# The planned duration of TensorE products is changed in a hand-ordered two-layer decoder kernel

## Chip, cores and metric

The kernel runs on one core of a Trainium2 chip. The metric is the device time of one execution in microseconds (us); lower is better. Engines are named as the profile names them: PE (TensorE matmul), PEld (TensorE weight load), DVE (VectorE), ACT (ScalarE), POOL (GpSimd), SP (SyncE, which issues the weight DMAs).

## What is computed

A decoder trunk of two layers over 256 tokens of width 1024, all in float32. Cut to its shape:

```python
for i in range(2):
    h = h + 0.5 * swiglu(rmsnorm(h), w_ff1_in[i], w_ff1_out[i])          # 1024 -> 2*2816 -> 1024
    u = rmsnorm(h)
    z = u @ w_in[i]             # [q | k | v | forget logits | conv GLU input | gate_attn | gate_conv]
    y_attn = forgetting_attention(q, k, v, f) @ w_attn_out[i]            # 8 heads x 64, causal
    y_conv = silu(rmsnorm(depthwise_conv31(a * sigmoid(b)))) @ w_conv_out[i]
    h = h + (sigmoid(ga) * y_attn + sigmoid(gc) * y_conv) @ w_out[i]
    h = h + 0.5 * swiglu(rmsnorm(h), w_ff2_in[i], w_ff2_out[i])
    h = h + sigmoid(rmsnorm(h) @ w_ple_gate[i]) * (p[i] @ w_ple_proj[i])
out = rmsnorm(h)
```

## The kernel before

Every float32 operand of a large product is split into two parts, high and low (`hi`, `lo`), and a product is three matmuls: high by high, high by low, low by high. Activations are held as `xs` (both parts side by side), weights come by DMA into `raw`, ACT copies the high part out (`whi`), and DVE subtracts it to get the low part (`wlo`). A weight block is mostly handled as two halves, each of 1024 columns per partition, and six half buffers (`WB`) exist for each of `whi` and `wlo`. So each weight half has to pass DMA, ACT and DVE before PE can use it.

The order of the instructions of each engine is written by a planner, the class `Flow`, when the program is built. It keeps a clock for PE, DVE and ACT, charges every operation a duration, and appends the operation that its clocks and priorities pick. `product` places a piece of large products on PE and moves PE's clock by `cost * len(items)`; `sides` lets small PE work (transposes, attention scores, attention values) in between two pieces once the planner believes its inputs are there. The engines then run their queues in exactly that order, each instruction waiting on semaphores for its real inputs; the planner's clocks themselves are not in the program. A duration in the planner therefore changes nothing but positions in the queues.

Three rules of the planner matter here. Splits of weights (`Weights.op`, `prio`) count how far a half is ahead of the half that PE's planned clock is on: less than one half ahead is priority 0.5, less than three (`AHEAD`) is 3, further ahead is 5. The 31 taps of the depthwise convolution are 124 DVE operations of each layer on the accumulator `acc`, with priority 4 (`conv_in`, `taps`): they fill DVE whenever the next halves are three ahead, and give way when they are not. Other DVE work (softmax maxima `nm`, splits of attention outputs) has priority 0 to 2 and goes first.

The mixer of a layer runs these large products in this order: convolution input, first half (`C0`); values and forget logits (`mm_vf`); convolution input, second half (below: C1); four blocks for queries and keys (below Q0, Q1, K0, K1; `mm_b`); eight blocks for the two gates (`mm_a`; the first is below GA0), with attention's scores, transposes and values placed between their pieces; the two output projections; `w_out`. Queries and keys are copied by ACT and then multiplied on POOL (`heads_out`, line 1035). A product on `mm_b` streams 256 columns three times, one on `mm_a` 512 columns three times, one on `mm_vf` 256 and 264 columns three times. The last line that the change touches is the planned duration of `values`, the small products of attention weights and values.

Everything that the helper class `Pinned` issues is recorded under line 285, so rows are told apart by the names of tiles: `mmps` and `xps` are the PSUM banks of PE, `wlo` and `whi` the weight parts, `acc` the convolution's accumulator.

Of the kernel before, what the change touches and what calls it, by code (L numbers as in the profile page):

```python
# [55 lines left out]
PE, V, A = "pe", "vector", "scalar"  # L56
# [7 lines left out]
def ac(n, ptr=0):  # L64
    return 95 + 0.834 * n + 90 * ptr
# [44 lines left out]
class Flow:  # L110
# [9 lines left out]
    def spawn(self, gen, at=None, prio=1, lat=LAT):  # L120
        self.seq += 1
        c = Chain(gen, prio, lat, self.seq)
        self.resume(c, self.t[PE] if at is None else at, None)
        return c.ev
# [290 lines left out]
def trunk(ctx: ExitStack, tc: tile.TileContext, x, p, g_ff1, w_ff1_in, w_ff1_out, g_mix, w_in, b_f,  # L415
# [116 lines left out]
    hT = keep.tile([P, KD, T], F32, name="hT")  # L532


    MB = 3 * 111

    def mm_b(ps, w, cols, xs, start, stop):
        hi, lo = w[0][:, cols], w[1][:, cols]
# [5 lines left out]
    def chunk(bank, m):  # L544
        return bank.t[:, m * T:(m + 1) * T]
# [4 lines left out]
    def items_b(blk, bank, m, k0, ks, kn, xs):  # L550
        return [(blk, k, (chunk(bank, m),), (slice(m * P, (m + 1) * P), xs[:, k0 + k], m == 0 and k0 + k == 0, m == 1 and k0 + k == kn - 1))
                for k in ks]


    def items_1(blk, ps, m, k0, ks, kn, xs):
        return [(blk, k, (ps,), (slice(m * P, (m + 1) * P), xs[:, k0 + k], k0 + k == 0, k0 + k == kn - 1)) for k in ks]


    MA = 3 * 217

    def mm_a(ps, xs, tt, w, start, stop):
        hi, lo = w
# [4 lines left out]


    VF = AW // 2
    MVF = 3 * (111 + 115)  # L570

    def mm_vf(ps, xs, tt, w, start, stop):
        for i, n in enumerate((VF, VF + H)):
# [2 lines left out]
    def piece(mm, cost, items, needs=()):  # L576

        hs = []
        for blk, k, *_ in items:
            if blk.of(k) not in hs:  # L580
                hs.append(blk.of(k))

        def run():
            for blk, k, before, after in items:
                mm(*before, blk.part(k), *after)
        for h in hs:
            wts.use(h)
        product(cost * len(items), run, list(needs) + [h.ready for h in hs])
# [198 lines left out]
    def ffn(wi, wo, norm, nxt, first=None):  # L787
# [3 lines left out]
        for k0 in range(0, KD, step):  # L791
            blks = [wts.take(wi, k0, step, c, 2 * P) for c in (0, FF)]
            for k in range(step):
                for i in range(2):
                    piece(mm_b, MB, [x for m in range(2) for x in items_b(blks[i], banks[i], m, k0, [k], KD, norm.xs)], [norm.ready[k0 + k]])
            wts.release(*blks)
# [3 lines left out]
        with tc.tile_pool(name="ffn", bufs=2) as ph, tc.tile_pool(name="ffn_g", bufs=1) as pg:  # L800
# [18 lines left out]
            for jj in range(KF // 2):  # L819
                if jj:  # L820
                    banks = []
                    for i in range(2):
# [3 lines left out]
                        for m in range(2):  # L826
                            for kk in range(0, KD, 4):
                                piece(mm_b, MB, items_b(blk, bank, m, 0, range(kk, kk + 4), KD, norm.xs))
                        wts.release(blk)
                spawn(glu(jj, *banks))  # L830
            for mm in range(KD // 2):
# [3 lines left out]
                for k0, kc in KPARTS:  # L835
                    blk = wts.take(wo, k0, kc, mm * 2 * P, 2 * P)
                    for m in range(2):
                        for h in blk.halves:
                            ks = range(h.a, h.b)
                            items = items_1(blk, hs[m].t[:, :T], m, k0, ks, KF, gs) if last else items_b(blk, hs[0], m, k0, ks, KF, gs)  # L840
                            piece(mm_b, MB, items, [ready[(k0 + k) // 2] for k in ks])
                        if k0 + kc == KF and last:
# [5 lines left out]
    def block_a(src, xs, kn, c0, needs):  # L848

        banks = [flow.take(mms) for _ in range(TT)]  # L850
        for k0 in range(0, kn, 4):
            blk = wts.take(src, k0, 4, c0, 512)
            for tt in range(TT):
                for h in blk.halves:
                    piece(mm_a_, MA, [(blk, k, (banks[tt].t, xs[:, k0 + k], tt), (k0 + k == 0, k0 + k == kn - 1))
                                      for k in range(h.a, h.b)], [needs[k0 + k] for k in range(h.a, h.b)])
# [6 lines left out]
    def mixer(l, norm, nxt):  # L863
        W = w_in[l]
        norm.root()
        with tc.tile_pool(name="mixer", bufs=1) as ph, tc.tile_pool(name="attn", bufs=2) as at:
# [66 lines left out]
            for k0 in range(0, KD, 4):  # L933
                blk = wts.take(W, k0, 4, V0, AW + H)
                for tt in range(TT):
                    for h in blk.halves:
                        piece(mm_vf, MVF, [(blk, k, (vbs[tt], norm.xs[:, k0 + k], tt), (k0 + k == 0, k0 + k == KD - 1))
                                           for k in range(h.a, h.b)], [norm.ready[k0 + k] for k in range(h.a, h.b)])
# [78 lines left out]
            def heads(c0, dst, scale):  # L1017
                evs = []
                for mm in range(AW // (2 * P)):
                    bank = flow.take(mms)  # L1020
                    blk = wts.take(W, 0, KD, c0 + mm * 2 * P, 2 * P)
                    for m in range(2):
                        for h in blk.halves:
                            ks = range(h.a, h.b)
                            piece(mm_b, MB, items_b(blk, bank, m, 0, ks, KD, norm.xs), [norm.ready[k] for k in ks])
                    wts.release(blk)
# [16 lines left out]
            def softmax(h0, qb, sch):  # L1043
                sc, kl = sch.t, (qb + 1) * P
                xp = yield xps
                pt = xp.t.rearrange("p (h k) -> p h k", h=2)

                def go():
                    for i in range(2):
                        tensor.matmul(out=pt[:, i, :kl], lhsT=QA[:, h0 + i, qb * P:(qb + 1) * P], rhs=KA[:, h0 + i, :kl],  # L1050
                                      start=True, stop=True)
                yield PE, 430 * (qb + 1), go
                yield A, ac(2 * kl), lambda: scalar.copy(out=sc, in_=pt[:, :, :kl])
                xp.free()

                diag = sc[:, :, qb * P:kl]
                nc.gpsimd.affine_select(out=diag, in_=diag, pattern=[[0, 2], [-1, P]], compare_op=ALU.is_ge, fill=NEG,
                                        base=0, channel_multiplier=1)
                yield flow.now + POOL
                nm = small.tile([P, 2], F32, name=f"nm{qb}")  # L1060
                sm = small.tile([P, 2], F32, name=f"sm{qb}")
                yield V, vc(2 * kl), lambda: vector.tensor_reduce(out=nm, in_=sc, axis=AX.X, op=ALU.max, negate=True)

                def exps():
                    for i in range(2):
                        scalar.activation(out=sc[:, i], in_=sc[:, i], func=AF.Exp, bias=nm[:, i:i + 1], accum_out=sm[:, i:i + 1])
                yield A, 2 * (ac(kl, 1) + 97), exps
                yield V, vc(2), lambda: vector.reciprocal(out=sm, in_=sm)

                def norms():  # L1070
                    for i in range(2):
                        scalar.activation(out=sc[:, i], in_=sc[:, i], func=AF.Copy, scale=sm[:, i:i + 1])
                yield A, 2 * ac(kl, 1), norms

            def attention(j):
                for e in have_qk:
                    yield e
                yield max(e.at for e in have_qk) + 2 * QK
                yield have_f
                h0 = 2 * j  # L1080
                sch = []
                for qb in range(TT):
                    h = yield scs[qb]
                    sch.append(h)
                evs = [spawn(softmax(h0, qb, sch[qb]), at=flow.now) for qb in range(TT)]
                for e in evs:
                    yield e
                exp_done[j].at = flow.now
                pT = yield pTs
                pbs = []  # L1090
                for i in range(2):
                    bank = yield mms
                    pbs.append(bank)

                def turned():
                    for i in range(2):
                        for n, part in enumerate((sch[0].t[:, i], sch[1].t[:, i, :P], sch[1].t[:, i, P:])):
                            tensor.transpose(out=pbs[i].t[:, n * P:(n + 1) * P], in_=part, identity=ident)
                yield PE, 660, turned
                for h in sch:  # L1100
                    h.free()
                for i in range(2):
                    yield A, ac(3 * P), lambda: scalar.copy(out=pT.t[:, 3 * i * P:3 * (i + 1) * P], in_=pbs[i].t[:, :3 * P])
                    pbs[i].free()
                yield have_v
                xp = yield xps
                po = xp.t[:, :T]

                def values():
                    for i in range(2):  # L1110
                        vh = slice((h0 + i) * DH, (h0 + i + 1) * DH)
                        o = po[i * DH:(i + 1) * DH]
                        q = pT.t[:, 3 * i * P:3 * (i + 1) * P]
                        tensor.matmul(out=o[:, 0:P], lhsT=v[:, 0, vh], rhs=q[:, 0:P], start=True, stop=True)
                        tensor.matmul(out=o[:, P:T], lhsT=v[:, 0, vh], rhs=q[:, P:2 * P], start=True, stop=False)
                        tensor.matmul(out=o[:, P:T], lhsT=v[:, 1, vh], rhs=q[:, 2 * P:], start=False, stop=True)
                yield PE, 700, values
                pT.free()
                yield from split((os_[:, j, :T], os_[:, j, T:]), po, T)
                xp.free()  # L1120
                os_ready[j].at = flow.now
# [67 lines left out]
            def w_out_part(hs, mm, k0, done=None):  # L1189
                blk = wts.take(w_out[l], k0, KC, mm * 2 * P, 2 * P)  # L1190
                for m in range(2):
                    items = items_b(blk, hs[0], m, k0, range(KC), KD, ms) if len(hs) == 1 else items_1(blk, hs[m].t[:, :T], m, k0, range(KC), KD, ms)
                    piece(mm_b, MB, items, ms_ready[k0 // KC])
                    if done:
# [40 lines left out]
    def ple(l, pT, have_p, norm, nxt, ph):  # L1235
# [8 lines left out]
        for mm in range(KD // 2):  # L1244
            bank = flow.take(mms)
            piece(mm_b, MB, [(blk, k, (chunk(bank, m),), (slice((2 * mm + m) * P, (2 * mm + m + 1) * P), pT[:, k], m == 0 and k == 0, m == 1 and k == 1))
                             for m in range(2) for k in range(2)], [have_p])
# [129 lines left out]
```

## Time and profile before

| | |
|---|---|
| median of 3 runs | 1161.68 us (1161.4 to 1162.49) |
| the profiled execution | 1161.82 us, its span 1160.0 us |
| mean granted TensorE clock | 0.995 |
| PE busy | 1141.9 us, 98% of the span, 8932 matmuls |
| DVE busy | 839.2 us, 72% |
| ACT busy | 615.4 us, 53% |
| POOL busy | 70.3 us, 6% |

The span is the time from the first to the last instruction; 1.8 us of the execution lie around it. Busy times are averages over the whole program, and the stages differ: the feed-forward stages and the mixer have to be read apart.

### The profile page before, as it was taken

Reading aid. Unit: us, or ns where it says so; the run is one execution under the profiler, and the core shown is the slowest. Engines: PE = TensorE matmul, PEld = TensorE weight load, DVE = VectorE, ACT = ScalarE, POOL = GpSimd, SP = SyncE. Lnnn points to the kernel's source line nnn. Section 1 sums busy time; section 2 is a strip of 40 time slices with the busy share of each in tenths; the row PEclk is TensorE's granted clock in tenths of the full one; section 3 lists DMA queues with packets and bytes.
Section 4 is the critical chain, followed back from the end, with each engine's and each line's share of the span. In section 5 each row is a group of like instructions: output and inputs, shape, how many; then the busy total and the mean of one; then the engine's idle time right before and its main releaser. Section 6 shows DMA issues by size and latency. Waiting matters only on the chain.

```text
span 1160.0 us, 21438 instructions
## 1 busy us (share of the span) xinstructions
PE 1141.9 (98%) x8932; PEld 1099.5 (95%) x8932; DVE 839.2 (72%) x1240; ACT 615.4 (53%) x906; POOL 70.3 (6%) x87
## 2 busy tenths in 40 slices
PE   8999999999999999999999999999999999999997
PEld 8999999888889999999999999999778999999997
DVE  7776555899986866655796665559998877665555
ACT  6544445657665444445654444456496455444454
POOL 1000001152000000000000000014410000000000
PEclk9999999999999999999999999999999999999999
DMA  9655556444547565565566555554344656655541
GB/s 295 220 181 182 170 194 198 132 147 144 182 149 249 174 202 182 169 201 177 162 200 221 181 174 181 192 192 154 129 133 152 216 186 213 201 178 178 191 145 38
DMA packets 189665, 207.70 MB, mean 179 GB/s; under 512 B 5000, under 2 KB 174048, under 8 KB 189568
## 3 DMA queue, kind: packets, MB, share of 16 engines
q1 hardware_dynamic: 188064, 205.60, 54.2%
q8 instruction: 70, 1.15, 0.4%
q0 software_dynamic: 1472, 0.72, 0.3%
q14 instruction: 27, 0.22, 0.1%
q10 hardware_dynamic: 32, 0.01, 0.0%
HBM read 205.23 MB, written 1.05 MB: 178 GB/s over the span
## 4 chain that ended last, share of the span: by engine, by line
PE 91%; DVE 5%; ACT 2%; issue 1%; DMA 0%; SPq 0%; DVEq 0%
PE mmps L285 81%; PE xps L285 10%; DVE acc L285 3%; DVE wlo L285 2%; ACT L285 1%; DMA xin<-in_x_dram 0%; ACT whi L285 0%; ACT sc L285 0%; ACT fe L285 0%; ACT t L285 0%; DVE t L285 0%; DVE nm L285 0%; SPq L349 0%; ACT v L285 0%; ACT fc L285 0%
## 5 line engine op out<-in xcount | busy, mean ns | idle before, releaser
L285 DVE TENSOR_TENSOR wlo<-raw,whi 128x1024 fp32r<-128x1024 f32 (+3 forms) x400 | 473.1, 1194 | 214.2 <-ACT whi L285 181.2
L285 PE MATMUL mmps<-xs,whi 128*128 128x256 f32 x3456 | 610.8, 281 | 0.0
L285 ACT CAST whi<-raw 128x1024 fp32r<-128x1024 f32 (+3 forms) x400 | 404.6, 1022 | 359.2 <-PE mmps L285 276.1
L285 PEld LDWEIGHTS mmps<-xs,whi 128*128 128x128 f32 x3456 | 528.8, 189 | 0.5
L285 PE MATMUL mmps<-xs,wlo 128*128 128x256 f32 x1728 | 483.7, 280 | 0.0
L285 PEld LDWEIGHTS mmps<-xs,wlo 128*128 128x128 f32 x1728 | 326.1, 189 | 0.0
L285 PE MATMUL mmps<-whi,xs 128*128 128x512 f32 (+2 forms) x640 | 195.0, 380 | 0.0
L285 PE MATMUL mmps<-gs,whi 128*128 128x256 f32 x1056 | 184.9, 279 | 0.0
L285 PEld LDWEIGHTS mmps<-gs,whi 128*128 128x128 f32 x1056 | 160.9, 188 | 0.0
L285 PE MATMUL mmps<-gs,wlo 128*128 128x256 f32 x528 | 147.5, 279 | 0.0
L285 PEld LDWEIGHTS mmps<-whi,xs 128*128 128x128 f32 x640 | 116.8, 189 | 22.3 <-issue 1.4
L285 PE MATMUL mmps<-wlo,xs 128*128 128x512 f32 (+1 forms) x320 | 119.6, 374 | 5.4 <-DVE wlo L285 5.4
L285 DVE SCALAR_TENSOR_TENSOR acc<-abuf,cols_taps,acc 128x256 f32<-128x256 f32 x240 | 114.8, 538 | 0.0
L285 PEld LDWEIGHTS mmps<-gs,wlo 128*128 128x128 f32 x528 | 99.4, 188 | 0.0
L285 PEld LDWEIGHTS mmps<-wlo,xs 128*128 128x128 f32 x320 | 60.6, 189 | 16.5 <-DVE wlo L285 6.9
L285 PE MATMUL xps<-gs,whi 128*128 128x256 f32 x352 | 61.7, 279 | 0.0
L285 ACT CAST gs<-a 128x512 fp32r<-128x512 f32 x44 | 27.4, 622 | 54.3 <-DVE a L285 54.3
L285 PEld LDWEIGHTS xps<-gs,whi 128*128 128x128 f32 x352 | 53.6, 188 | 0.0
L285 PE MATMUL xps<-gs,wlo 128*128 128x256 f32 x176 | 49.2, 279 | 0.0
L285 ACT ACTIVATE xs<-hT,cols_mix 128x256 fp32r<-128x256 f32 (+1 forms) x56 | 28.2, 505 | 23.8 <-DVE hT L285 23.8
L870 POOL MEMSET QA<- 2x2048 f32 x2 | 3.6, 1804 | 611.0 <-PE xps L285 611.0
L285 DVE SCALAR_TENSOR_TENSOR hT<-mmps,hT 128x512 f32<-128x512 f32 x18 | 12.4, 691 | 35.6 <-PE mmps L285 35.6
(142 smaller groups left out, 790.0 us busy)
## 6 DMA issues: line engine op xcount, KB each, us to landing
raw<-in_w_ff_in_dram SPq DMA_DIRECT2D x80, 1024.0 KB, 5.1
raw<-in_w_ff_out_dram SPq DMA_DIRECT2D x32, 896.0 KB, 4.8
raw<-in_w_in_dram SPq DMA_DIRECT2D x24, 1024.0 KB, 5.2
raw<-in_w_ff_out_dram SPq DMA_DIRECT2D x16, 1024.0 KB, 5.2
raw<-in_w_in_dram SPq DMA_DIRECT2D x16, 512.0 KB, 4.5
raw<-in_w_out_dram SPq DMA_DIRECT2D x16, 512.0 KB, 3.7
raw<-in_w_ple_gate_dram SPq DMA_DIRECT2D x8, 1024.0 KB, 5.2
raw<-in_w_ff_in_dram SPq DMA_DIRECT2D x12, 512.0 KB, 4.0
```

Of the source, the lines that this page charges most:

```text
L285: return self.tc.keep_in_program_order(f(*a, **k))
L870: nc.gpsimd.memset(QA[DH:DH + 2], 1.0)
```

## The change

Four durations that the planner charges are replaced. No instruction, tile or buffer is added or removed; each engine gets the same operations, in whatever order the planner writes with the new numbers.

```diff
-    MB = 3 * 111
+    MB = 351
...
-    MA = 3 * 217
+    MA = 693
...
-    MVF = 3 * (111 + 115)
+    MVF = 717
...
-                yield PE, 700, values
+                yield PE, 1075, values
```

The old values are 333, 651 and 678 ns for one product (one item) of each kind, so an item is charged 18, 42 and 39 ns more, and one round of `values` 375 ns more. The durations charged to DVE, ACT and POOL stay.

## Rows read from the trace of the kernel before

**Rows 1.** The page's first part: busy us, share of the span, instructions.
```profile
PE 1141.9 (98%) x8932; PEld 1099.5 (95%) x8932; DVE 839.2 (72%) x1240; ACT 615.4 (53%) x906; POOL 70.3 (6%) x87
```

**Rows 2.** What PE waited for: us in total, times, longest us.
```profile
PE mmps L285 <- DVE wlo L285: 5.4, 4, 2.0
PE mmps L285 <- DMA xin<-in_x_dram: 2.2, 1, 2.2
...
PE mmps L285 <- ACT sc L285: 1.1, 1, 1.1
```

**Rows 3.** One 20 us stretch of a feed-forward stage: busy us (instructions), clock, DMA.
```profile
400.00:420.00 20.00, 20.00 (x174) 20.00 (x173) 14.06 (x16) 8.85 (x10) 0.00 (x0) 1.00 0.63 202
```

**Rows 4.** Timeline of PE, layer 0: start us, us, operation, [idle before].
```profile
213.85 0.28 PE L285 MATMUL mmps<-wlo,xs 128*128 128x264 f32 x1
...
219.61 0.28 PE L285 MATMUL mmps<-wlo,xs 128*128 128x264 f32 x1
...
255.91 0.50 PE L285 MATMUL mmps<-wlo,xs 128*128 128x512 f32 x1 [0.69 <-DVE wlo L285]
...
259.57 0.50 PE L285 MATMUL mmps<-wlo,xs 128*128 128x512 f32 x1 [2.00 <-DVE wlo L285]
...
298.39 1.15 PE L285 MATMUL xps<-pT,v 128*64 128x128 f32 x12
...
302.58 0.40 PE L285 MATMUL mmps<-wlo,xs 128*128 128x512 f32 x1
...
310.19 0.39 PE L285 MATMUL mmps<-wlo,xs 128*128 128x512 f32 x1
```

**Rows 5.** Timeline of PE in the last stage, products of 256 columns.
```profile
1139.87 0.28 PE L285 MATMUL mmps<-xs,wlo 128*128 128x256 f32 x1
...
1142.69 0.28 PE L285 MATMUL mmps<-xs,wlo 128*128 128x256 f32 x1
```

**Rows 6.** Timeline of DVE in the mixer of layer 0.
```profile
214.27 0.73 DVE L285 TENSOR_SCALAR acc<-abuf,cols_taps,cols_mix 128x256 f32<-128x256 f32 x2 [2.41 <-ACT abuf L285]
214.92 5.62 DVE L285 SCALAR_TENSOR_TENSOR acc<-abuf,cols_taps,acc 128x256 f32<-128x256 f32 x14
...
227.05 0.41 DVE L285 TENSOR_TENSOR fl<-fl,fe 8x256 f32<-8x256 f32 x1 [0.29 <-ACT fe L285]
...
233.29 0.43 DVE L285 SCALAR_TENSOR_TENSOR t<-t,t 128x256 f32<-128x256 f32 x1 [0.26 <-ACT t L285]
...
237.88 2.35 DVE L285 TENSOR_TENSOR wlo<-raw,whi 128x1024 fp32r<-128x1024 f32 x2
240.15 7.42 DVE L285 SCALAR_TENSOR_TENSOR acc<-abuf,cols_taps,acc 128x256 f32<-128x256 f32 x8
247.50 2.35 DVE L285 TENSOR_TENSOR wlo<-raw,whi 128x1024 fp32r<-128x1024 f32 x2
249.77 4.96 DVE L285 SCALAR_TENSOR_TENSOR acc<-abuf,cols_taps,acc 128x256 f32<-128x256 f32 x7
254.64 1.22 DVE L285 TENSOR_TENSOR wlo<-raw,whi 128x1024 fp32r<-128x1024 f32 x1
...
257.22 2.29 DVE L285 TENSOR_TENSOR wlo<-raw,whi 128x1024 fp32r<-128x1024 f32 x1
```

**Rows 7.** Timeline of POOL in the same stretch.
```profile
238.88 3.94 POOL L1035 TENSOR_TENSOR QA<-QA,rall 64x512 f32<-64x512 f32 x2 [0.71 <-ACT QA L285]
```

**Rows 8.** Stretches of 4 us, columns as in rows 3: layer 0, then layer 1.
```profile
258.00:262.00 4.00, 2.43 (x7) 1.97 (x8) 4.00 (x8) 0.12 (x1) 0.43 (x1) 0.78 0.29 75
262.00:266.00 4.00, 4.00 (x17) 3.29 (x17) 4.00 (x8) 1.22 (x2) 0.00 (x0) 0.80 0.48 187
...
830.00:834.00 4.00, 4.00 (x21) 3.38 (x21) 4.00 (x7) 0.41 (x1) 0.00 (x0) 1.00 0.64 238
```

**Rows 9.** Timeline of PE in the mixer of layer 1.
```profile
828.33 0.50 PE L285 MATMUL mmps<-wlo,xs 128*128 128x512 f32 x1 [2.01 <-DVE wlo L285]
...
843.56 0.84 PE L285 MATMUL mmps<-ident,sc 128*128 128x128 f32 x5 [1.07 <-ACT sc L285]
```

## The prediction, made before the changed kernel had run

> **What bounds the kernel now.** I began with the page's busy times: PE is busy 1141.9 of 1160.0 us, so 18.1 us are all that an order without any wait could win [rows 1]. The stretches of 20 us tell where those lie: in the feed-forward stages PE is busy for the whole of each stretch while DVE is busy 14.06 of 20 us [rows 3], so no order there is short of anything. The list of PE's waits names the low weight parts from DVE first: 5.4 us in four waits, the longest 2.0 us; a wait for attention scores takes 1.1 us, and the first input's 2.2 us at the start belongs to the first load [rows 2]. The timeline of PE puts two of the four waits at 255.91 and 259.57 us, 0.69 and 2.00 us long, at the first gate block of layer 0 [rows 4]; the one of 2.01 us at 828.33 us is their like in layer 1 [rows 9]. The reader should see that the kernel is PE's work plus these stumbles, and that the change touches no work, so only the stumbles can move.
>
> Why PE stumbles there is in DVE's timeline [rows 6]. From 214.27 us DVE works through taps and weight splits with hardly a gap. Fourteen taps take 5.62 us, 0.40 us each; a split takes 1.14 us (two from 237.88 to 240.15 us). But the eight taps from 240.15 us take 7.42 us, 0.93 us each, and the next seven 4.96 us. In that stretch POOL multiplies queries and keys [rows 7]. DVE so falls behind the order's plan, and the two splits that the first gate block needs, at 254.64 and 257.22 us, come after PE wants them.
>
> **Are the new numbers those of the trace?** In the last stage nine low-part matmuls start from 1139.87 to 1142.69 us, eight products of 256 columns: 0.353 us each [rows 5]; charged 0.333, then 0.351. On `mm_a` twelve start from 302.58 to 310.19 us, so eleven products take 0.692 us each; charged 0.651, then 0.693. On `mm_vf` nine of those with 264 columns start from 213.85 to 219.61 us, eight items of 0.720 us; charged 0.678, then 0.717. A round of values takes about 1.15 us; charged 0.70, then 1.075 [rows 4]. So the planner has been charging PE about 5 to 6% too little, and afterwards it charges about right.
>
> **What that does to the order.** A weight half is split when PE's planned clock reaches a given earlier half; taps fill what DVE time the plan leaves between. With a PE that is planned too fast, the plan leaves DVE less time than it really gets, and this unplanned slack pays for what the planner doesn't know, POOL's interference above all. With the right durations every block leaves DVE more planned time, and as taps always stand ready in this stretch, it goes to taps. So more taps come ahead of the split that PE waits for.
>
> The sum for layer 0, from the first tap at 214.27 us to the planned start of block K1, from where the two late splits are ordered. What is left of `mm_vf` is (219.61 + 0.72 - 214.27) / 0.72, or 8.4 items, by 39 ns: 0.33 us. C1 has two blocks of eight items (four rows of k by two token tiles) by 42 ns: 0.67 us. Q0, Q1 and K0 have 16 items each (eight rows of k by two column tiles), 48 by 18 ns: 0.86 us. Together 1.86 us, or 4.7 more taps of 0.395 us. On a DVE that is never idle after 214.27 us they delay both splits, and so PE, by all of it. DVE did stand idle 0.29 and 0.26 us in this stretch [rows 6]; taps that fall there cost nothing, so the term lies between 1.3 and 1.9 us a layer. I take 1.7, nearer the full sum, since the order fixes who waits and not every tap finds a gap: 3.4 us for two layers, on top of the 2.7 us that each waits now.
>
> The price of a tap has two ends: 0.40 us by its own row, and 0.93 us where POOL works beside it [rows 6, 7]. By the dear end 4.7 taps cost 4.4 us a layer. I take the cheap end: POOL's work isn't lengthened, and the excess of the eight slow taps (7.42 less 8 by 0.40, 4.2 us) is about the time of POOL's instructions beside them, 3.94 us for the first pair. [...]
>
> **Behind the stumble.** After 259.57 us PE and DVE start again with no slack. Eight gate blocks of eight items by 42 ns are 2.7 us more of planned time, and four rounds of values 1.5 us more. Scores and the later splits are covered now: no wait for `wlo` follows in either layer. What is late next is attention. In layer 1 PE waits 1.07 us at 843.56 us for scores out of the softmax, 13.9 us of PE work after the stumble's end [rows 9]. About 10 us of that are gate products; planned 6% longer, some 0.6 us fewer of them stand ahead of these transposes, so the wait grows by about 0.6 us. [...] I take 0.6 us in all; bounds 0 and 2.4 us (0.6 for each of four such places).
>
> **The clock.** [...] Net 0.6 us; bounds 0 and 3.4 us (1.7 in each layer).
>
> Nothing else is charged. In the feed-forward and the last stages the other orders hide behind PE, DVE having about 6 of 20 us free [rows 3]. DMA issues keep their sequence. If that cover failed, a single split of 1.14 us would be the unit of cost.
>
> **Sum.** 3.4 + 0.6 + 0.6 = 4.6 us on the profiled execution's 1161.82 us: 1166.4 us. That execution is 0.1 us above the median of the runs, so 1166.3 us, 0.4% slower.
>
> **Rivals.** *Nothing measurable* (within 0.2% or 2.3 us, which is also about what a measurement can tell from no change): the extra taps fall into gaps. Beside the 0.55 us there are 2.41 us of idle DVE ahead of the first tap [rows 6]; if the order's first taps come earlier by as much as the plan lengthens, the splits keep their real times. Against it: the first tap hangs on a convolution input that PE itself has to turn, and that position is planned by the same clock. It gives 1161.7 us, with 0 to 2 us added.
>
> *Slower by more*: the added taps meet POOL at 0.93 us. Twice 4.4 plus 1.2 us is 10.0 us, 1171.7 us. It decides if every tap that runs while POOL works is slowed, however many there are. Against it: eight such taps lost in all about what one pair of POOL's instructions lasted [rows 6, 7].
>
> *Faster*: a whole group of taps changes places with the pair of splits. The seven taps from 249.77 us stand ahead of the two late splits [rows 6]. Choices fall at the bounds of pieces of PE work, so a small change of clock can put the pair ahead of the group instead. If the pair comes 2.7 us earlier, three of these slow taps, the stumble is gone: 2.7 us in each layer and 1.7 us of clock, 7.1 us in all, 1154.6 us; half of it, one layer, would be 1158. Against it: longer products shift splits the other way, and it needs a reversal, not a shift.
>
> **Chances and range.** Forecast (1163.5 to 1169) 0.48; no change 0.25; dearer taps 0.10; faster 0.17. The range has to reach down to the no-change case and a little below, and up beyond the clock's bound: 1159 to 1171 us leaves out most of the faster case and half of the dear one, about 2 in 10. Slower by over 0.2%: 0.58; within: 0.25; faster: 0.17.
>
> **What would show it.** Right: PE's work as before; the waits of PE for `wlo` near 10 us, not 5.4, at the same two places; four or five more taps between 214 and 257 us in layer 0; the granted clock below 1 in layer 1 after its stumble; the wait for scores in layer 1 unchanged or longer. The taps end earlier in each layer, with nothing won, because no wait stands there now. Wrong: the same or fewer taps ahead of the splits of the first gate block, or PE waits elsewhere, as for PSUM banks in a feed-forward stage. What I could most easily have wrong is that the planner fills the added time with taps: its choices are discrete, and one group that moves is worth more than the whole sum.

## The result and the profile after

The changed kernel takes 1177.79 us (median of 4 runs, 1175.45 to 1177.9) where the kernel before took 1162.09 us beside it (4 runs, 1161.4 to 1164.21): ratio 1.0127, 95% interval 1.0113 to 1.0141. It is slower, as forecast, but by 15.7 us and not by 4.6.

The profiled span is 1175.7 us, 15.7 more than before. PE's busy time and its list of waits divide that. First the page's busy line of the changed kernel (its counterpart is [rows 1]):

```profile
PE 1147.2 (98%) x8932; PEld 1103.9 (94%) x8932; DVE 826.3 (70%) x1240; ACT 616.9 (52%) x906; POOL 107.3 (9%) x87
```

PE is busy 5.3 us longer with the same 8932 matmuls. POOL is busy 37.0 us longer with the same 87 instructions, while DVE is busy 12.9 us less. Next PE's waits in the changed kernel, columns as in [rows 2]:

```profile
PE xps L285 <- POOL KA L1035: 17.2, 4, 8.2
PE mmps L285 <- DMA xin<-in_x_dram: 1.9, 2, 1.1
PE xps L285 <- ACT sq L285: 1.1, 1, 1.1
PE mmps L285 <- DVE eps L285: 1.1, 1, 1.1
```

The waits for `wlo` and for scores are gone, and one wait for POOL's keys stands in their place. All waits come to 21.3 us, against 10.9 in the whole list of before: 10.4 us more, which with the 5.3 us of busy time make the 15.7. The timeline of PE in the changed kernel shows where it stands in layer 0:

```profile
259.87 0.40 PE L285 MATMUL mmps<-whi,xs 128*128 128x512 f32 x1
268.43 0.80 PE L285 MATMUL xps<-KA,QA 66*128 66x128 f32 x2 [8.16 <-POOL KA L1035]
269.65 2.50 PE L285 MATMUL xps<-KA,QA 66*128 66x128 f32 x6 [0.42 <-POOL KA L1035]
```

Layer 1 has the same waits, 8.17 and 0.42 us. In stretches of 4 us (columns as in [rows 3]) the granted clock falls with the wait, from 0.78 to 0.50, and is 0.50 and 0.51 until 276 us, where before it was 0.78 and 0.80 for 8 us [rows 8]. Of the 7.2 us that PE is busy from 268 to 276 us about half, 3.6 us, is lost to it (an estimate from these rows); with the like in layer 1 that is more than enough for the 5.3 us of busy time:

```profile
260.00:264.00 4.00, 0.27 (x2) 0.00 (x0) 3.60 (x8) 0.00 (x0) 4.00 (x1) 0.78 0.70 247
264.00:268.00 4.00, 0.00 (x0) 0.00 (x0) 0.00 (x0) 0.00 (x0) 4.00 (x4) 0.50 0.00 0
268.00:272.00 4.00, 3.15 (x9) 2.49 (x10) 0.00 (x0) 0.37 (x1) 4.00 (x4) 0.50 0.00 0
272.00:276.00 4.00, 4.00 (x13) 3.33 (x12) 2.71 (x5) 2.70 (x8) 1.07 (x3) 0.51 0.00 0
276.00:280.00 4.00, 4.00 (x19) 3.27 (x19) 3.42 (x10) 4.00 (x16) 1.11 (x2) 1.00 0.76 259
```

Between 264 and 268 us only POOL works. So the question is what POOL did until then. POOL's timeline in the changed kernel answers to [rows 7]:

```profile
238.69 28.47 POOL L1035 TENSOR_TENSOR QA<-QA,rall 64x512 f32<-64x512 f32 x4
267.12 4.92 POOL L1035 TENSOR_TENSOR KA<-KA,rall 64x512 f32<-64x512 f32 x4
```

POOL starts at 238.69 us, as it did before (238.88). But the four multiplications of queries take 28.47 us together, in place of 1.4 to 2.5 us each, and those of keys 1.25 us each once it is 267 us. The view by source line has the extremes over both layers (minimum, median, maximum in ns):

```profile
L1035 POOL TENSOR_TENSOR QA<-QA,rall x8: 1252/5153/17098, 238.7 to 841.6; 64x512 f32<-64x512 f32 x8
L1035 POOL TENSOR_TENSOR KA<-KA,rall x8: 1255/1257/1260, 267.1 to 846.5; 64x512 f32<-64x512 f32 x8
```

DVE's timeline of the changed kernel shows what runs beside them, and answers to [rows 6]:

```profile
232.35 1.20 DVE L285 TENSOR_TENSOR wlo<-raw,whi 128x1024 fp32r<-128x1024 f32 x1
233.49 0.41 DVE L285 SCALAR_TENSOR_TENSOR t<-t,t 128x256 f32<-128x256 f32 x1
...
240.73 3.24 DVE L285 SCALAR_TENSOR_TENSOR acc<-abuf,cols_taps,acc 128x256 f32<-128x256 f32 x8
...
246.17 3.24 DVE L285 SCALAR_TENSOR_TENSOR acc<-abuf,cols_taps,acc 128x256 f32<-128x256 f32 x8
249.33 1.20 DVE L285 TENSOR_TENSOR wlo<-raw,whi 128x1024 fp32r<-128x1024 f32 x1
250.47 0.47 DVE L285 SCALAR_TENSOR_TENSOR acc<-abuf,cols_taps,acc 128x256 f32<-128x256 f32 x1
250.86 1.20 DVE L285 TENSOR_TENSOR wlo<-raw,whi 128x1024 fp32r<-128x1024 f32 x1
252.00 2.05 DVE L285 SCALAR_TENSOR_TENSOR acc<-abuf,cols_taps,acc 128x256 f32<-128x256 f32 x5
253.97 1.87 DVE L285 TENSOR_SCALAR acc<-abuf,cols_taps,cols_mix 128x256 f32<-128x256 f32 x2
...
262.74 0.86 DVE L285 SCALAR_TENSOR_TENSOR acc<-abuf,cols_taps,acc 128x256 f32<-128x256 f32 x2
272.44 0.42 DVE L285 TENSOR_REDUCE nm<-sc 128x2 f32<-128x256 f32 x1 [8.84 <-POOL sc L1057]
```

Three things are to be seen. Eight taps take 3.24 us, not 7.42: POOL doesn't slow them. (Of the 124 taps of layer 0 one takes 1.5 us, the second of the two at 253.97 us.) The two splits of the first gate block start at 249.33 and 250.86 us, not at 254.64 and 257.22. And the idle 0.26 us that before stood ahead of the first gated product `t` at 233.29 us is gone: `t` follows the split at once. The first multiplication, which begins at 238.69, takes 17.0 us and ends only at 255.69 us, during the two taps at 253.97, which start a new accumulator and so have one input tile in place of two; the second needs 9.1 us more and is done after DVE has run out of work at 263.6 us. The reading that follows, for these instructions, is: beside a DVE that never waits, POOL doesn't get through.

### The profile page after: what moved, and what is told of

Read it like the earlier page. It is cut to its first block, busy times and chain, and to the rows that moved or that the text cites. A ratio compares the mean times of both kernels' runs of the same rounds, so it can differ in the third digit from the quotient of the medians.

```text
span 1175.7 us, 21440 instructions
## 1 busy us (share of the span) xinstructions
PE 1147.2 (98%) x8932; PEld 1103.9 (94%) x8932; DVE 826.3 (70%) x1240; ACT 616.9 (52%) x906; POOL 107.3 (9%) x87
## 4 chain that ended last, share of the span: by engine, by line
PE 89%; POOL 4%; issue 4%; DMA 1%; SPq 0%; ACT 0%; DVE 0%; DVEq 0%; POOLq 0%
PE mmps L285 79%; PE xps L285 10%; POOL QA L1035 3%; DMA xin<-in_x_dram 1%; DMA KA<-fc 0%; POOL KA L1035 0%; SPq L349 0%; POOL KA L984 0%; POOL QA L983 0%; POOL KA L871 0%; SPq L453 0%; ACT L285 0%; DVE o L285 0%; DVEq L1372 0%; ACT QA L285 0%
## 5 line engine op out<-in xcount | busy, mean ns | idle before, releaser
L285 DVE SCALAR_TENSOR_TENSOR acc<-abuf,cols_taps,acc 128x256 f32<-128x256 f32 x240 | 100.5, 475 | 0.0
L1035 POOL TENSOR_TENSOR QA<-QA,rall 64x512 f32<-64x512 f32 x8 | 57.0, 7153 | 0.2 <-ACT QA L285 0.2
```

The source lines that it names most:

```text
L285: return self.tc.keep_in_program_order(f(*a, **k))
L1035: nc.gpsimd.tensor_tensor(out=part, in0=part, in1=norm.rall[:DH].unsqueeze(1).to_broadcast([DH, 2, T]), op=ALU.mult)
```

## The experiments

Theory A (theory 1, or the theory, in the expectations): POOL's multiplication is kept waiting as long as DVE's instructions follow each other without a wait; the longer plan has filled DVE's last wait ahead of it (for ACT's `t`), and so the keys come late. Theory B: the changed order of DVE's work itself (more taps ahead of the splits) makes the loss, and POOL's long durations are a companion. Each ratio is to the kernel before, run on the same chip.

**Pauses for DVE.** Behind each multiplication of the changed kernel the planner waits 1.5 us and places a small DVE copy that reads its result, so that DVE has to stop for POOL:

```diff
                     nc.gpsimd.tensor_tensor(out=part, ...)
+                    yield flow.now + 1500
+                    peek = small.tile([DH, 1], F32, name="peek")
+                    yield V, vc(1), lambda: vector.tensor_copy(out=peek, in_=part[:, 0, 0:1])
```

> The changed kernel with one tiny DVE instruction behind each of POOL's multiplications of queries and keys, which reads one column of the result, so that DVE stops until POOL is done. Theory 1 (POOL's multiplication does not get started while DVE issues taps and splits back to back; in the changed order it was held for 17 and 9 us, and PE waited 8.2 us for the keys): each multiplication takes under 3 us again, PE's wait for POOL is gone, and the time falls from 1177.8 to 1158 to 1166 us. Rival (more taps stand ahead, DVE is simply late): DVE gets still more to do, the time stays at 1177 us or rises.

1170.56 us, ratio 1.0074 (1.0059 to 1.0089). The multiplications of queries take 1.28 to 3.36 us, and PE has no wait for POOL left; but it waits 6.7 us for scores, 4.2 us for `wlo` and 1.8 us for the copies. So POOL's delay yields to stops of DVE. The time came out above the range that was expected: the three waits named last make 12.7 us in place of the 17.2 for POOL.

**No POOL at all.** The same multiplication on DVE, planned with its own cost:

```diff
-                    nc.gpsimd.tensor_tensor(out=part, in0=part, in1=norm.rall[:DH]..., op=ALU.mult)
+                    yield V, vc(2 * T), lambda: vector.tensor_tensor(out=part, in0=part, in1=norm.rall[:DH]..., op=ALU.mult)
```

> The changed kernel with the eight multiplications of queries and keys of each layer on DVE and not on POOL, planned as DVE work. Theory 1: nothing is left that DVE can hold up, PE's wait for POOL is gone, 1155 to 1164 us. Rival (DVE is late): 8 times 0.69 us more on a DVE that is full in this stretch, 5.5 us a layer, so 1180 us or more, with waits for wlo.

1150.7 us (1150.52 to 1150.82), ratio 0.9905 (0.9888 to 0.9922): faster than both kernels, and below the range that was expected. The whole list of PE's waits in this run:

```profile
PE mmps L285 <- DMA xin<-in_x_dram: 2.0, 3, 0.9
PE xps L285 <- ACT sq L285: 1.1, 1, 1.1
PE mmps L285 <- DVE eps L285: 1.1, 1, 1.1
```

Nothing is left in either mixer. A multiplication takes DVE 0.67 us, as its timeline in this run shows, and the taps beside it stay at 0.40:

```profile
243.65 1.21 DVE L285 TENSOR_TENSOR wlo<-raw,whi 128x1024 fp32r<-128x1024 f32 x1
244.79 0.68 DVE L285 TENSOR_TENSOR QA<-QA,rall 64x512 f32<-64x512 f32 x1
...
247.13 2.05 DVE L285 SCALAR_TENSOR_TENSOR acc<-abuf,cols_taps,acc 128x256 f32<-128x256 f32 x5
```

**Which duration.** The kernel before with one or two of the four new numbers:

```diff
-    MB = 3 * 111
+    MB = 351
```

> The kernel before with the one duration MB = 351 changed. If the loss comes from the order within the stretch of queries and keys (MB is charged there), POOL's multiplications are held as in the changed kernel, and the time is 1172 to 1178 us. If it takes the longer charge of the convolution input and the gates, the time is within 4 us of 1162 us.

```diff
-    MA = 3 * 217
+    MA = 693
```

> The kernel before with the one duration MA = 693 changed. If the loss comes from the stretch of queries and keys alone, nothing is held on POOL and the time is within 4 us of 1162 us; by the sum of the prediction 0.67 us more of planned time in C1 and 2.7 us behind the stumble are worth 1163 to 1165 us. If POOL is held here too, 1172 us or more.

```diff
-    MVF = 3 * (111 + 115)
+    MVF = 717
...
-                yield PE, 700, values
+                yield PE, 1075, values
```

> Before with the two other durations alone: 717 for values and forget logits, 1075 for a round of attention values. If POOL's exclusion in layer 0 comes with the longer plan of the gates (MA) alone, POOL's multiplications stay under 4 us here and the time is 1160 to 1165 us. If any longer plan that closes DVE's wait for ACT's `t` will do, a multiplication takes over 5 us and the time is 1168 us or more. If the parts add up, the time is that of the change less the two others: 15.7 less 3.4 less 10.7, or 1.6 us over before.

`MB` alone: 1165.49 us, ratio 1.0027 (1.0017 to 1.0038), POOL's multiplications at most 3.6 us, the idle time ahead of `t` still there. `MA` alone: 1172.41 us, ratio 1.0092 (1.0077 to 1.0107), no idle time ahead of `t`, the longest multiplication 23.8 us, and this first row of PE's waits:

```profile
PE xps L285 <- POOL KA L1035: 14.6, 4, 7.1
```

The other two: 1162.53 us, ratio 1.0003 (0.9994 to 1.0013), multiplications of at most 1.5 us. Counted in DVE's timelines, 29 taps stand ahead of the split that leads to `t` before and with `MB` alone, 30 with the last two numbers, 31 with `MA` alone and 32 in the changed kernel. POOL is held with 31 and 32 and not with 29 and 30. `MA` is the one that plans C1, the convolution input just ahead of `t`.

**The changed order with one short wait of DVE.** A copy of one column on ACT and one on DVE that waits for it, unplanned, behind the second `t`; the order of everything else is the changed kernel's:

```diff
...
+                        if cc[0] and tt == 1:
+                            g0 = small.tile([P, 1], F32, name="g0")
+                            g1 = small.tile([P, 1], F32, name="g1")
+                            scalar.copy(out=g0, in_=ones[:, 0:1])
+                            vector.tensor_copy(out=g1, in_=g0)
...
```

> The changed kernel with one copy of one column on ACT and one on DVE that waits for it, right behind the second product t of the second convolution input of each layer, both outside the plan: the order of everything else stays. Theory 1 (as long as DVE has not once waited, its instructions follow each other without a hole and POOL's multiplication isn't let in; a single short wait of DVE before the stretch of queries and keys opens it): DVE waits some 0.3 to 0.6 us at about 235 us, POOL's multiplications take under 4 us each, PE's wait for POOL is gone, and what is left is the stumble on wlo and scores of the prediction: 1162 to 1169 us. Rival (the taps that stand ahead hold DVE and so POOL, whatever DVE waits for): POOL is held as before, 1177 us or more.

1168.66 us, ratio 1.0064 (1.0049 to 1.0079). DVE's timeline of this run:

```profile
235.80 0.15 DVE L285 COPY g<-g 128x1 f32<-128x1 f32 x1 [0.24 <-ACT g L285]
...
243.45 5.32 DVE L285 SCALAR_TENSOR_TENSOR acc<-abuf,cols_taps,acc 128x256 f32<-128x256 f32 x8
...
256.20 1.22 DVE L285 TENSOR_TENSOR wlo<-raw,whi 128x1024 fp32r<-128x1024 f32 x1
257.34 1.51 DVE L285 SCALAR_TENSOR_TENSOR acc<-abuf,cols_taps,acc 128x256 f32<-128x256 f32 x1
258.77 2.29 DVE L285 TENSOR_TENSOR wlo<-raw,whi 128x1024 fp32r<-128x1024 f32 x1
```

and POOL's, and PE's three first waits in layer 0:

```profile
238.86 3.58 POOL L1042 TENSOR_TENSOR QA<-QA,rall 64x512 f32<-64x512 f32 x2
244.36 2.93 POOL L1042 TENSOR_TENSOR QA<-QA,rall 64x512 f32<-64x512 f32 x2 [1.92 <-ACT QA L285]
```

```profile
249.96 0.39 PE L285 MATMUL mmps<-xs,wlo 128*128 128x256 f32 x1 [0.48 <-DVE wlo L285]
257.47 0.50 PE L285 MATMUL mmps<-wlo,xs 128*128 128x512 f32 x1 [1.62 <-DVE wlo L285]
261.11 0.51 PE L285 MATMUL mmps<-wlo,xs 128*128 128x512 f32 x1 [1.99 <-DVE wlo L285]
```

A wait of 0.24 us at 235.80 us, 3 us before POOL's first multiplication, lets POOL in again; eight taps pay for it with 5.32 us, and PE stumbles over `wlo` and not over keys. 9.1 of the 15.7 us go (1177.79 less 1168.66). What is left, 7.0 us over the 1161.66 us of before beside it, is what this order costs where POOL is let in. In the spans it is 6.4 us: 2.8 more of waits for `wlo`, 2.7 for scores, 0.6 for the first input, 0.3 of busy time. The copy with its wait is part of that, about 0.4 us of DVE's time a layer (the tap behind it starts 0.71 us after `t`; with nothing between, 0.34). It isn't a price that the order has without POOL: with the multiplication on DVE (planned anew) PE waits in neither mixer. So both theories hold a part, and the larger is A's. The added copy has one input, which a rival might blame in place of the wait; but before has the wait at `t` without such a copy, and the one-input taps of the changed kernel are followed by taps as short as ever (0.465 us at 255.77).

**The order of before without that wait.** The converse: DVE work put ahead of the first `t` of the second convolution input, first one addition of 128x256 elements (about 0.33 us), then three:

```diff
...
+                        if cc[0] and tt == 0:
+                            junk = small.tile([P, T], F32, name="junk")
+                            vector.tensor_tensor(out=junk, in0=hT[:, 0], in1=hT[:, 1], op=ALU.add)
                         vector.scalar_tensor_tensor(out=av.t[:, :T], ...)
```

> The kernel before with one addition of 128 by 256 elements put in front of the first product t of the second convolution input of each layer, outside the plan, so that DVE no longer idles 0.26 us there; the order of everything else stays. Theory 1: without that wait POOL's first multiplication is held for more than 5 us as in the changed kernel, PE waits for POOL, 1170 us or more. Rival (DVE's lateness alone counts): 0.4 us more on DVE in each layer, at most 1163 us, POOL as before.

> Before with three DVE additions of 128x256 (about 1.1 us) ahead of the first gated product `t` of the second convolution input in each layer, in the queue's order only; the plan's durations are the old ones. Theory (a DVE that has not once waited keeps POOL out): ACT's `t` has then long arrived, DVE goes on without any idle time, taps after it take 0.465 to 0.470 us instead of 0.476 to 0.479, a multiplication of POOL takes over 5 us, PE waits for keys or queries from POOL, and the time is 1168 us or more, although only some 1.1 us of DVE work was added in each layer. Rival (it takes another sequence of instructions, the lost wait is not the cause): multiplications on POOL stay under 4 us, PE's waits for the low weight parts grow by at most about 1 us in each layer, and the time is 1161 to 1164.5 us.

1161.79 us, ratio 1.0003 (0.9993 to 1.0013), and 1163.8 us, ratio 1.0014 (1.0004 to 1.0024). Neither held POOL up (its longest multiplications 2.5 and 3.2 us), against theory A's numbers. In the second run the additions follow at 0.44 and 0.46 us where 0.335 us would be close, so DVE had holes of 0.1 us between them, and taps after `t` took 0.478 us. In the first, the addition is close to its split within 0.003 us and `t` to the addition, yet the taps after `t` take 0.477 us as before. ACT's times, the first line below, tell more: ACT's part of `t` ends at 233.31 us in that run, and DVE's `t` starts 0.04 us behind it; before, where DVE plainly waited for it, the distance is 0.03 us. So `t` most likely still waited there, hidden under the end of the addition, and that run took no wait away. With three additions the distance is 0.95 us, so there only the holes are left to open the way for POOL. These are the lines of the run with one addition, ACT's and then DVE's:

```profile
232.47 0.84 ACT L285 ACTIVATE t<-mmps,rhalf 128x256 f32<-128x256 f32 x2
233.01 0.41 DVE L285 TENSOR_TENSOR junk<-hT 128x256 f32<-128x256 f32 x1
233.35 0.41 DVE L285 SCALAR_TENSOR_TENSOR t<-t,t 128x256 f32<-128x256 f32 x1
```

The next run adds a single longer instruction, and the distance is 0.58 us:

```diff
-                            junk = small.tile([P, T], F32, name="junk")
-                            vector.tensor_tensor(out=junk, in0=hT[:, 0], in1=hT[:, 1], op=ALU.add)
+                            junk = small.tile([P, 3, T], F32, name="junk")
+                            vector.tensor_tensor(out=junk, in0=hT[:, 0:3], in1=hT[:, 1:4], op=ALU.add)
```

> Before with one DVE addition of 128x768 (about 0.9 us, one instruction, so no hole of its own) ahead of the first gated product `t` of the second convolution input in each layer, in the queue's order only. In the run with three separate additions each addition began about 0.1 us late behind the one before, so DVE was not without holes there and that run settled nothing. Theory (a DVE that goes on without a hole keeps POOL out): `t` follows without idle time, the taps after it take 0.465 to 0.470 us, a multiplication of POOL takes over 5 us, and the time is 1167 us or more. Rival (another sequence, not the lost wait, is the cause): the taps after `t` take 0.476 to 0.480 us as before, POOL's multiplications stay under 4 us and the time is 1161 to 1164.5 us.

1172.19 us, ratio 1.0094 (1.0077 to 1.0111). DVE's timeline of this run, then POOL's, then the first of PE's waits:

```profile
231.51 1.21 DVE L285 TENSOR_TENSOR wlo<-raw,whi 128x1024 fp32r<-128x1024 f32 x1
232.64 0.94 DVE L285 TENSOR_TENSOR junk<-hT 128x768 f32<-128x768 f32 x1
233.51 0.41 DVE L285 SCALAR_TENSOR_TENSOR t<-t,t 128x256 f32<-128x256 f32 x1
...
240.37 3.24 DVE L285 SCALAR_TENSOR_TENSOR acc<-abuf,cols_taps,acc 128x256 f32<-128x256 f32 x8
```

```profile
238.57 27.10 POOL L1040 TENSOR_TENSOR QA<-QA,rall 64x512 f32<-64x512 f32 x4 [0.76 <-ACT QA L285]
265.64 4.92 POOL L1040 TENSOR_TENSOR KA<-KA,rall 64x512 f32<-64x512 f32 x4
```

```profile
PE xps L285 <- POOL KA L1040: 14.3, 4, 6.7
```

With the plan, the order and the taps of before, 0.94 us of work in place of a wait of 0.26 us makes the same picture: packed taps, held multiplications, PE waiting for keys. So for this place nothing of the changed order is needed: with no wait and no hole on DVE from 229 us on POOL is held (its longest multiplication here 20.2 us), and with either it is let in (at most 2.5 us with the wait of before, 3.2 with the holes).

**The order of before without POOL** (the multiplication on DVE, the edit of *No POOL at all* on the kernel before), and the changed kernel with the multiplication taken into the copy out of PSUM, one DVE instruction in place of ACT's and POOL's:

```diff
-                    yield A, ac(2 * T), lambda: scalar.activation(out=part, in_=chunks(bank)[...], func=AF.Copy, scale=scale)
-                    nc.gpsimd.tensor_tensor(out=part, in0=part, in1=norm.rall[:DH]..., op=ALU.mult)
+                    yield V, vc(2 * T), lambda: vector.scalar_tensor_tensor(out=part, in0=chunks(bank)[...], scalar=scale, in1=norm.rall[...]..., op0=ALU.mult, op1=ALU.mult)
```

> The kernel before with the multiplications of queries and keys on DVE, planned as DVE work, as the changed kernel had them in the run at 1150.7 us. If POOL's interference was all that the four durations changed, both orders now run alike: 1149 to 1153 us. If the longer durations do something of their own, as the prediction's sum says (3.4 us more waiting for splits in the changed order), this one is 2 us or more faster, 1148 us or less; if right durations help once POOL is out of the way, it is slower than 1152 us.

> The changed kernel with copy and multiplication of queries and keys in one DVE instruction out of PSUM, so that ACT's eight copies and POOL's eight multiplications of each layer fall away. ACT was no limit, so about the 1150.7 us of the run with the multiplication on DVE, 1149 to 1152 us; if a late copy on ACT still held DVE or the banks, up to 2 us faster.

1164.81 us, ratio 1.0027 (1.0017 to 1.0038), and 1151.6 us, ratio 0.9914 (0.9899 to 0.9928). So with POOL out of the way the old durations give 1164.81 us and the new ones 1150.7: there the change is worth 14 us, with the other sign, the last of the outcomes that were expected. With the old durations PE waits 7.4 us more (11.6 against 4.2 us in all) and is busy 6.8 us longer (1143.9 against 1137.1). The two largest waits of layer 0 lie behind the end of the taps:

```profile
324.97 0.68 PE L285 MATMUL xps<-ident,rtok 128*128 128x128 f32 x4 [1.75 <-DVE rtok L285]
327.81 0.80 PE L285 MATMUL mmps<-whi,xs 128*128 128x512 f32 x1 [2.16 <-ACT xs L285]
```

The last tap of layer 0 ends at 315.3 us in that run, with the new durations at 305.7. That the late taps cause these two waits was only read from the trace, not tried.

## Why the prediction was wrong, step by step

- *The new numbers are those of the trace; PE's work stays.* Right: the same 8932 matmuls, and the durations of `values` and `mm_vf` by themselves change nothing that can be measured.
- *More taps come ahead of the late splits, 4.7 in a layer.* Right: 56 and 57 taps stand ahead of the two splits in layer 0, before 51 and 52.
- *They delay the splits by 1.7 us, and PE's waits for `wlo` grow by 3.4 us.* Right where POOL is let in: with the short wait put back the splits start at 256.20 and 258.77 us, 1.6 us later than in [rows 6], and `wlo` costs 8.2 us in all, 2.8 more than in [rows 2]. But about 0.4 us of the 1.6 is the added copy and its wait, and two of the six waits, 0.48 us each, stand at a place that wasn't forecast, the last block of keys (249.96 us).
- *Attention waits 0.6 us more.* Under-sized: in that run scores cost 3.8 us in place of 1.1, 2.7 more, just over the upper bound of 2.4.
- *The clock falls in layer 1 as well, net 0.6 us.* Half right, but no run shows a term of 0.6 us: in that run the clock is 0.75 and 0.82 from 832 to 840 us, but 1.00 throughout layer 0's stretch (252 to 276 us), and PE's busy time grows by 0.3 us. The unit of 1.7 us a layer, also in the rival *faster*, was the author's estimate, 8 us at 0.78 and 0.80 of the full clock [rows 8]. It was too large: of those 8 us PE is busy for 6.43, so the loss there is 1.3 us (an estimate from the same rows).
- *The price of a tap: "POOL's work isn't lengthened".* **This is the step that failed.** It read [rows 6, 7] as a loss that is fixed by POOL's instructions and always falls on DVE. For the kernel before that is so, though not as the rows were added up: of the eight taps of 7.42 us four take 1.50 to 1.53 us and four 0.47, so no tap costs 0.93 us, and the excess of 4.2 us belongs to four multiplications, not to the first pair. In the changed kernel it fell on POOL: one multiplication of 17.0 us and one of 9.1 in layer 0 (17.1 and 9.1 in layer 1), DVE's taps at 0.40 us, keys late by 8.2 us a layer, the clock at 0.50 behind it. The first waits that the prediction named, for `wlo`, disappeared, since DVE was faster by 12.9 us. The rival *dearer taps* (1171.7 us) failed too, though its time is the nearest of those named: but for one in each layer, no tap was dear.

The trace of before shows how the two engines hold each other up: a tap takes 1.50 to 1.53 us beside a multiplication and 0.47 us without one, and the multiplications of queries and keys in layer 0 take 1.3 to 2.5 us, where one takes 1.25 us in the changed kernel once DVE is idle. The prediction's step needs more, that POOL gets its turn between two DVE instructions; here it got none between 28 DVE instructions with two inputs (239.20 to 253.97 us in the changed kernel), all of which began after the multiplication's recorded start at 238.69 us. So in this case POOL's earlier start did not give it the first turn, and this is what the runs put in place of the step.

That the forecast had the sign right is in good part luck. The mechanism that it argued is worth at most 7 of the 15.7 us (4.6 forecast), and in the changed kernel itself its waits, for `wlo` and scores, don't occur; the slowdown measured there came by the way that the prediction had ruled out, with 9.1 us that go when POOL is let in.

## What to carry to other kernels

A model that is corrected in one place can lose an error that covered another: here the too short PE durations, that of `mm_a` above all, left DVE a wait of 0.26 us, and POOL lived on it (its longest multiplication 2.5 us before, 17.1 us in the changed kernel). Where two engines hold each other up, a row that shows one of them paying isn't a price: ask which of them pays when the other never stops, and look at who waits for each. When a right number makes a kernel slower, try taking away the hidden partner (here one POOL instruction, moved to DVE and charged to it in the plan) before taking back the number: the two together are 0.95% faster than before, each alone is slower.

## What the runs showed of the hardware

A multiplication of 64x512 elements on POOL takes 1.25 us beside an idle DVE, 1.3 to 3.6 us where DVE has waited once some 3 to 6 us before the first of them, and up to 17.1 us (the changed kernel) or 23.8 us (`MA` alone) beside a DVE that hasn't. The two cases can be told apart before POOL starts, in DVE's own durations: taps of 0.465 to 0.470 us and splits of 1.20 to 1.21 us where POOL is later held, 0.476 to 0.481 and 1.21 to 1.22 us where it gets in, with the same spacing of 0.396 us from tap to tap. Holes of 0.1 us were enough (three additions). Not every wait does it: before, DVE waits 0.29 us at 227.05 us, and the tap behind takes 0.468 us. And the durations change without a wait too: in layer 0 of both kernels taps take 0.476 to 0.483 us until the one instruction that reads `fl` out of PSUM (224.71 us before, 225.22 after), and 0.463 to 0.469 us behind it. So what told the runs apart is a wait or a hole at `t` or just around it, and none that came earlier. Why it still counts at 239 us, and what in the end decides who goes first, stays open; so does why the first multiplication got in at two one-input taps in the changed kernel (253.97 us), in the run with the long addition (257.47 us) and in layer 1 of the run with `MA` alone, and not in that run's layer 0.
